# Copying gate matrices out of PSUM on VectorE instead of ScalarE after the last selection, with the gates' pace counted for it

## The chip, the cores and the metric

The kernel runs on one NeuronCore of a Trainium2 chip. Its five engines (TensorE, VectorE, ScalarE, GpSimd and SyncE, in the profile PE, DVE, ACT, POOL and SP) each work through a queue of their own in order and wait for one another by semaphores. The metric is the device time of one execution in microseconds (us), lower is better.

## The reference

One layer of a diffusion backbone over 512 latent tokens and 256 context tokens, D = 1024. The mixers come first; the part that matters here is the feed-forward at the end, PEER, in which each token retrieves 128 of 16384 one-neuron experts (8 heads, 16 each):

```python
half_s, half_i = lax.top_k(s, PEER_TOPK)               # scores against two sets of 128 keys
cand = half_s[:, :, 0, :, None] + half_s[:, :, 1, None, :]
best_s, best_c = lax.top_k(cand.reshape(...), PEER_TOPK)
experts = i1 * PEER_KEYS + i2
gate = jax.nn.softmax(best_s, axis=-1)
act = jax.nn.gelu(jnp.einsum('td,thkd->thk', hb, u_table[experts]))
return jnp.einsum('thk,thkd->td', gate * act, v_table[experts])
```

## The kernel before, in words

For 384 of the 512 tokens PEER is computed densely: all 16384 experts are taken in 128 blocks of 128. The *first product* of a block (`first_product`, 24 matmuls of 384 columns, tile `pa`) gives the activations of its experts for all 384 tokens, and the *second product* (18 matmuls of 512 columns, tiles `pacc`) adds activation times gate times v. The remaining 128 tokens gather their own rows of u and v (`gather_u`, `gather_v`): GpSimd fetches 128 rows of 4 KB at a time into `grow`, VectorE takes a dot product of it (L1452).

The dense gates must be built: `gate_matrices` makes, for four tokens at a time (a *set*), one-hot matrices on VectorE (`h1` at L1429, `o2` at L1431), scales `h1` by the gate on ScalarE (`o1`, four ACTIVATE at L1433), multiplies them on TensorE into a PSUM tile `pm` (L1439), and copies that into `stg` (L1440), whose token index is the innermost one: the copy reads `pm` in a row and writes elements that lie 32 floats, 128 bytes, apart. There are 96 sets; eight fill one `stg`, and a full `stg` is written to `Gd` in DRAM by four DMAs that ScalarE's queue issues (L1445). Matmul and copy of a set stand two sets behind its one-hots (`GLAG = 2`); `pm` has two buffers.

The stage in question is a loop over blocks (`while nb < NBLK and (not gm.done or nb % GRP)`). One iteration transposes the u of the block two further on (`transpose_u`: DVE L1486, ACT cast `w_hi` L1487, POOL `w_lo` in two halves L1491), issues a first product, writes its activations to `Ad` in DRAM, and then runs three side programs by budgets in us: gathers, gate matrices (`gm`) and selections (`tk`, one for each 128 tokens). A side program gets its budget added to what it is owed, and runs pieces until their `yield`s have used it up; `spent` counts the work handed out. Once the three selections are done (`tk.done`), `stage[0]` becomes 1 and the gates' budget per block becomes `GMX`. The loop ends at the first multiple of 4 blocks at which all 96 sets are done: 112 here. The other 16 blocks go through a *second loop* over turns n = 0 to 132: there a turn does the first product of a block that is left (if one is) and, five turns behind, the second product of a block; blocks that went through the first loop come last there and read `Ad` back. `Gd` is read in groups of eight blocks (`gg`).

The orders of VectorE and GpSimd are those of the program text (`manual_schedule`); TensorE, ScalarE and SyncE are ordered by a scheduler when the kernel is built. Iterations and blocks are counted from 0 below, sets from 1; iteration i of the first loop opens with the transpose for block i + 2, written T(i + 2).

Of the kernel before, what the change touches and what calls it, by code (L numbers as in the profile page):

```python
# [55 lines left out]
TK0 = 10  # L56
TK1 = 30
SLACK = 10
GMX = 3.3
GU2 = 1.6  # L60
TKORD = [0, 1, 2]
PRI = 3000
# [73 lines left out]
def body(ctx: ExitStack, tc: tile.TileContext, I, out, dbg=lambda *a: None):  # L136
    nc = tc.nc
    V, S, G, PE, SP = nc.vector, nc.scalar, nc.gpsimd, nc.tensor, nc.sync
# [56 lines left out]
    def psum(tag="a", name="pt"):  # L195
        return ps.tile([P, 512], F32, name=name, tag=tag, bufs={"a": 2, "s": 3, "o": 1}[tag])
# [49 lines left out]
    pt = psum()  # L246
    PE.transpose(pt[:, :16], crow2, ident[:16, :16])
    V.tensor_copy(vcol[:, :16], pt[:, :16])
    pt = psum()
# [30 lines left out]
    for k in range(KC):  # L280
        for i in range(3):
            if i % 2 == 0:
                pt = psum("as"[n // 2 % 2])
# [105 lines left out]
    pt = psum()  # L389
# [686 lines left out]
    ready, now, spent, stage = {}, [0], [0.0, 0.0], [0]  # L1076
# [148 lines left out]
    for h in range(4):  # L1225
        szh = gate_tile(16 + h)
        pt = psum()
# [15 lines left out]
    for h0 in range(0, HEADS, 4):  # L1243
        pt = psum()
# [156 lines left out]
    def pkt(shape, name, dt=F32, bufs=1):  # L1401
        return pk.tile(shape, dt, name=name, tag=name, bufs=bufs)
# [13 lines left out]
    def gate_matrices(l):  # L1416

        while l not in ready or now[0] < ready[l][0] + MWAIT:
            yield 0.0
        i1, i2, gT = ready[l][1:]  # L1420
        held = []
        for t0 in range(0, P, TB):
            stg = pkt([P, KEYS, TB], "stg", bufs=2)
            for t in range(t0, t0 + TB + 4 * GLAG, 4):
                busy = t < t0 + TB
                if busy:
                    if t % OT == 0:
                        h1 = pkt([P, P, OT], "h1", BF, bufs=GLAG + 1)
                        V.tensor_tensor(h1, iotab, i1[:, None, t:t + OT].to_broadcast([P, P, OT]), op=ALU.is_equal)  # L1429
                    o2, o1 = pkt([P, 4, P], "o2", bufs=GLAG + 1), pkt([P, 4, P], "o1", bufs=GLAG + 1)  # L1430
                    V.tensor_tensor(o2, io[0][:, None, :].to_broadcast([P, 4, P]), i2[:, t:t + 4, None].to_broadcast([P, 4, P]), op=ALU.is_equal)  # L1431
                    for j in range(4):
                        S.activation(o1[:, j], h1[:, :, t % OT + j], AF.Copy, scale=gT[:, t + j:t + j + 1])  # L1433
                    held.append((t, o1, o2))
                if len(held) > GLAG or not busy:
                    tp, o1, o2 = held.pop(0)
                    pt = ps.tile([P, 512], F32, name="pm", tag="m", bufs=2)
                    for j in range(4):
                        PE.matmul(pt[:, j * P:(j + 1) * P], o2[:, j], o1[:, j], start=True, stop=True)  # L1439
                    S.copy(stg[:, :, tp - t0:tp - t0 + 4].rearrange("p i t -> p t i"), pt.rearrange("p (t i) -> p t i", t=4))  # L1440
                    spent[0] += 0.9
                yield 1.1 if busy else 0.01
            pc = (l * P + t0) // TB
            for i0 in range(0, KEYS, 32):
                S.dma_start(Gd[pc, :, i0:i0 + 32], stg[:, i0:i0 + 32])  # L1445
# [32 lines left out]
    def transpose_u(b):  # L1478
# [13 lines left out]
        return tuple(x.rearrange("p (k f) -> p k f", f=P) for x in (hi, lo))  # L1492

    gm = Side(chain(gate_matrices(0), gate_matrices(1), gate_matrices(2)))
    spent[:] = [0.0, 0.0]
    gu = Side(chain(gather_u(), gather_v()))
# [11 lines left out]
    while nb < NBLK and (not gm.done or nb % GRP):  # L1508
# [13 lines left out]
        if tk.done and not stage[0]:  # L1522
            stage[0] = 1
        gm.run(GM if not tk.done else GMX)
        if not tk.done:
# [166 lines left out]
```

## Time and profile before

| | |
|---|---|
| median of three runs | 2057.54 us (2054.82 to 2059.9) |
| the profiled execution: time, span | 2055.5 us, 2053.7 us |
| TensorE (matmul) busy over the span | 1912.8 us, 93% |
| VectorE busy | 1637.4 us, 80% |
| ScalarE busy | 951.4 us, 46% |
| GpSimd busy | 978.9 us, 48% |
| granted TensorE clock, mean | 0.975 of full speed |

Shares over the whole span are means over very different stages: the mixers fill the first 790 us, the first loop runs from there to some 1417 us, the second to the end. A stage is read by its own rows. A time such as 1304.76 is counted from the start of the span.

### The profile page before, as it was taken

The numbers are of one execution on the slowest core, as the hardware profiler recorded it, in microseconds if no ns is written. First come the engines' busy times: TensorE is split into PE (matmuls) and PEld (weight loads), VectorE is DVE, ScalarE is ACT, GpSimd is POOL, SyncE is SP. The second block draws the span as 40 slices with busy tenths as digits, with TensorE's granted clock in tenths as the row PEclk, the third lists the DMA queues.
The fourth block names the chain that finished last, engine by engine and source line by source line (L and its number), as shares of the span: only waits on it lengthen the run. The fifth ranks groups of instructions, "written<-read, shape, count | busy, mean of one in ns | idle before, by whom it ended". The sixth has DMA issues, their size and how long they took to land.

```text
span 2053.7 us, 29600 instructions
## 1 busy us (share of the span) xinstructions
PE 1912.8 (93%) x10018; PEld 1622.3 (79%) x10018; DVE 1637.4 (80%) x3311; ACT 951.4 (46%) x1770; POOL 978.9 (48%) x695
## 2 busy tenths in 40 slices
PE   7999999999898997999999999989889999999997
PEld 2766667788786796889999999889777888888885
DVE  4599885377766659899998999666779888989886
ACT  4455554333332443333666666797323333333333
POOL 2755444311212872677666566443345545545430
PEclk9999999999999998999999999999999999999999
DMA  9333332422425785889888888788999999999992
GB/s 311 93 113 109 109 92 83 128 84 62 125 68 175 214 199 157 240 234 257 246 248 261 248 249 247 228 280 286 300 311 356 390 357 399 381 379 380 393 389 87
DMA packets 283477, 475.87 MB, mean 232 GB/s; under 512 B 35224, under 2 KB 197293, under 8 KB 282813
## 3 DMA queue, kind: packets, MB, share of 16 engines
q1 hardware_dynamic: 214251, 277.82, 44.5%
q0 software_dynamic: 36864, 134.23, 19.2%
q10 hardware_dynamic: 32210, 61.93, 8.4%
q8 instruction: 79, 1.29, 0.3%
q14 instruction: 73, 0.60, 0.1%
HBM read 409.71 MB, written 64.18 MB: 231 GB/s over the span
## 4 chain that ended last, share of the span: by engine, by line
PE 37%; POOL 9%; DMA 6%; issue 6%; ACT 6%; DVE 4%; ACTq 1%; SPq 1%; DVEq 0%; POOLq 0%
PE pacc L174 8%; PE pacc L175 8%; PE pacc L173 8%; POOL w_lo L1491 6%; PE pa L175 3%; PE pa L173 3%; PE pa L174 3%; DMA w_raw<-in_peer_u_dram 3%; ACT o L1433 2%; ACT stg L1440 2%; PE pm L1439 2%; POOL grow L1459 2%; POOL w_lo L169 1%; ACT w_hi L1487 1%; DMA w_raw<-in_peer_wq_dram 1%
## 5 line engine op out<-in xcount | busy, mean ns | idle before, releaser
L1491 POOL TENSOR_TENSOR w_lo<-ut,w_hi 128x512 fp32r<-128x512 f32 x224 | 294.6, 1338 | 229.0 <-ACT w_hi L1487 223.3
L173 PE MATMUL pa<-h2T_hi,w_hi 128*128 128x384 f32 x1024 | 355.5, 347 | 38.9 <-ACT w_hi L1487 36.1
L175 PE MATMUL pa<-h2T_hi,w_lo 128*128 128x384 f32 x1024 | 360.0, 353 | 8.5 <-POOL w_lo L1491 6.9
L174 PE MATMUL pa<-h2T_lo,w_hi 128*128 128x384 f32 x1024 | 349.7, 341 | 0.0
L169 POOL TENSOR_TENSOR w_lo<-w_raw,w_hi 128x1024 fp32r<-128x1024 f32 x78 | 198.5, 2557 | 301.7 <-ACT w_hi L168 222.0
L1470 POOL DMA_INDIRECT grow<-in_peer_v_dram,exi x128 | 205.0, 1601 | 211.6 <-DVE accg L1474 190.1
L1573 ACT CAST w_hi<-w_raw 128x1024 fp32r<-128x1024 f32 x124 | 130.5, 1053 | 244.7 <-PE pacc L175 89.2
L173 PEld LDWEIGHTS pa<-h2T_hi,w_hi 128*128 128x128 f32 x1024 | 198.1, 193 | 46.6 <-ACT w_hi L1487 46.1
L175 PEld LDWEIGHTS pa<-h2T_hi,w_lo 128*128 128x128 f32 x1024 | 197.8, 193 | 14.5 <-POOL w_lo L1491 11.1
L174 PE MATMUL pacc<-w_lo,wh 128*128 128x512 f32 x744 | 194.6, 396 | 9.2 <-DVE w_lo L1577 9.2
L1459 POOL DMA_INDIRECT grow<-in_peer_u_dram,exi x128 | 148.6, 1161 | 104.8 <-DVE act L1452 85.2
L174 PEld LDWEIGHTS pa<-h2T_lo,w_hi 128*128 128x128 f32 x1024 | 197.6, 193 | 0.3
L175 PE MATMUL pacc<-w_hi,wl 128*128 128x512 f32 x744 | 193.7, 395 | 0.0
L173 PE MATMUL pacc<-w_hi,wh 128*128 128x512 f32 x744 | 193.7, 395 | 0.0
L1487 ACT CAST w_hi<-ut 128x1024 fp32r<-128x1024 f32 x126 | 132.4, 1052 | 131.1 <-DVE ut L1486 105.0
L174 PEld LDWEIGHTS pacc<-w_lo,wh 128*128 128x128 f32 x744 | 139.0, 188 | 44.9 <-DVE w_lo L1577 12.0
L1577 DVE TENSOR_TENSOR w_lo<-w_raw,w_hi 128x1024 fp32r<-128x1024 f32 x124 | 151.3, 1220 | 22.9 <-ACT w_hi L1573 22.8
L175 PEld LDWEIGHTS pacc<-w_hi,wl 128*128 128x128 f32 x744 | 139.7, 188 | 33.9
L173 PEld LDWEIGHTS pacc<-w_hi,wh 128*128 128x128 f32 x744 | 139.6, 188 | 33.9
L1486 DVE STREAM_TRANSPOSE ut<-w_raw 128x1024 f32<-128x1024 f32 x126 | 155.6, 1237 | 12.6 <-DMA w_raw<-in_peer_u_dram 10.7
L1474 DVE SCALAR_TENSOR_TENSOR accg<-grow,act,accg 128x1024 f32<-128x1024 f32 x127 | 162.4, 1279 | 3.2 <-DMA grow<-in_peer_v_dram,exi 2.2
L173 PE MATMUL pg<-hL_hi,w_hi 128*128 128x512 f32 (+1 forms) x336 | 139.7, 416 | 0.0
(450 smaller groups left out, 4092.9 us busy)
## 6 DMA issues: line engine op xcount, KB each, us to landing
w_raw<-in_peer_u_dram SPq DMA_DIRECT2D x512, 128.0 KB
w_raw<-in_peer_v_dram SPq DMA_DIRECT2D x128, 512.0 KB
Gd<-stg ACTq DMA_DIRECT2D x48, 512.0 KB
gg<-Gd SPq DMA_DIRECT2D x16, 1536.0 KB
Ad<-ga ACTq DMA_DIRECT2D x112, 192.0 KB
aa<-Ad SPq DMA_DIRECT2D x28, 768.0 KB
w_raw<-in_w_ada_dram SPq DMA_DIRECT2D x40, 512.0 KB
w_raw<-in_w_in_dram SPq DMA_DIRECT2D x34, 512.0 KB
```

The source lines that it names most:

```text
L169: (lo_eng or G).tensor_tensor(lo, raw, hi.bitcast(F32), op=ALU.subtract)
L173: PE.matmul(o, lh, rh, start=start, stop=False)
L174: PE.matmul(o, lh, rl, start=False, stop=False)
L175: PE.matmul(o, ll, rh, start=False, stop=stop)
L1459: G.indirect_dma_start(out=u, out_offset=None, in_=UT_, in_offset=bass.IndirectOffsetOnAxis(ap=exi[:, j:j + 1], axis=0))
L1470: G.indirect_dma_start(out=v, out_offset=None, in_=VT_, in_offset=bass.IndirectOffsetOnAxis(ap=exi[:, j:j + 1], axis=0))
L1474: V.scalar_tensor_tensor(accg, v, act[:, j:j + 1], accg, op0=ALU.mult, op1=ALU.add)
L1486: V.transpose(lf.rearrange("p (c f q) -> p c f q", f=4, q=32), u.rearrange("p f (c x) -> p c f x", x=32))
L1487: S.copy(hi, lf)
L1491: eng.tensor_tensor(lo[:, cs], lf[:, cs], hi[:, cs].bitcast(F32), op=ALU.subtract)
L1573: S.copy(vh, v)
L1577: V.tensor_tensor(vl, v, vh.bitcast(F32), op=ALU.subtract)
```

## The change

Once the last selection is done, VectorE's `tensor_copy` takes the place of ScalarE's `copy` for a set, and a set's `yield` is 1.7 (before 1.1), a copy without new one-hots 0.6 (before 0.01). The budget for each block becomes 4.4 (before 3.3).

```diff
-GMX = 3.3
+GMX = 4.4
...
-                    S.copy(stg[:, :, tp - t0:tp - t0 + 4].rearrange("p i t -> p t i"), pt.rearrange("p (t i) -> p t i", t=4))
+                    (V.tensor_copy if stage[0] else S.copy)(stg[:, :, tp - t0:tp - t0 + 4].rearrange("p i t -> p t i"),
+                                                            pt.rearrange("p (t i) -> p t i", t=4))
                     spent[0] += 0.9
-                yield 1.1 if busy else 0.01
+                yield (1.7 if stage[0] else 1.1) if busy else 0.6 if stage[0] else 0.01
```

What the planner makes of it: sets 55 to 96 are copied by VectorE, 42 in all. Eight sets now use 14.8 us of budget, that is 3.4 blocks, where they used 8.8 us or 2.7 blocks. All sets are done at block 116, not 112, so 116 blocks pass through the first loop and 12 are left to the second, where it was 112 and 16; and the first group that the second loop reads from `Gd` has four blocks (0.75 MB), not eight (1.5 MB).

VectorE's order in an iteration late in the first loop, before. `ut` is the transpose, the two ISA rows are one dot product and its sum, `h1` and `o2` the one-hots:

```order
L1486 STREAM_TRANSPOSE ut_13146<-w_raw_13139 128x1024
L1452 ISA grow_12995,act_6998<-grow_12995,h2p_7008 128x1024
L1452 ISA act_6998 128x1
L1429 TENSOR_TENSOR h1_13182<-iop_7010,i1_12584 128x512
L1431 TENSOR_TENSOR o2_13184<-iop_7010,i2_12585 128x512
L1429 TENSOR_TENSOR h1_13197<-iop_7010,i1_12584 128x512
L1431 TENSOR_TENSOR o2_13199<-iop_7010,i2_12585 128x512
L1429 TENSOR_TENSOR h1_13212<-iop_7010,i1_12584 128x512
L1431 TENSOR_TENSOR o2_13214<-iop_7010,i2_12585 128x512
L1486 STREAM_TRANSPOSE ut_13234<-w_raw_13227 128x1024
```

And now, the end of iteration 104 (its transpose and two dots stand ahead; `pm_13199` is set 72, the last of a `stg`, and `pm_13237` is set 73) and the start of iteration 105:

```order
L1453 ISA act_6998 128x1
L1440 COPY stg_12906<-pm_13199 128x4x128
L1429 TENSOR_TENSOR h1_13210<-iop_7010,i1_12584 128x512
L1431 TENSOR_TENSOR o2_13212<-iop_7010,i2_12585 128x512
L1429 TENSOR_TENSOR h1_13219<-iop_7010,i1_12584 128x512
L1431 TENSOR_TENSOR o2_13221<-iop_7010,i2_12585 128x512
L1429 TENSOR_TENSOR h1_13228<-iop_7010,i1_12584 128x512
L1431 TENSOR_TENSOR o2_13230<-iop_7010,i2_12585 128x512
L1440 COPY stg_13209<-pm_13237 128x4x128
L1487 STREAM_TRANSPOSE ut_13250<-w_raw_13243 128x1024
```

The copies stand between the one-hots, and the next block's transpose now stands behind a copy, which waits for a matmul.

TensorE's order around the copies of sets 73 to 75, now. `pa_13328` is the first product of block 106, whose transpose opened iteration 104, and `pa_13416` that of block 107:

```order
L174 MATMUL pa_13328<-h2T_lo_5733,w_hi_13158 128x384
L175 MATMUL pa_13328<-h2T_hi_5732,w_lo_13159 128x384
L173 MATMUL pa_13328<-h2T_hi_5732,w_hi_13158 128x384
L174 MATMUL pa_13328<-h2T_lo_5733,w_hi_13158 128x384
L175 MATMUL pa_13328<-h2T_hi_5732,w_lo_13159 128x384
L1439 MATMUL pm_13237<-o1_13213,o2_13212 128x128 x4
L1439 MATMUL pm_13295<-o1_13222,o2_13221 128x128 x4
L1439 MATMUL pm_13310<-o1_13231,o2_13230 128x128 x4
L173 MATMUL pa_13416<-h2T_hi_5732,w_hi_13248 128x384
```

Before (`pa_13239` is block 104, whose transpose opened iteration 102, `pa_13330` block 105; the sets 73 and 74 were made in iteration 102):

```order
L173 MATMUL pa_13239<-h2T_hi_5732,w_hi_13051 128x384
L174 MATMUL pa_13239<-h2T_lo_5733,w_hi_13051 128x384
L175 MATMUL pa_13239<-h2T_hi_5732,w_lo_13052 128x384
L1439 MATMUL pm_13191<-o1_13124,o2_13123 128x128 x4
L173 MATMUL pa_13330<-h2T_hi_5732,w_hi_13144 128x384
L174 MATMUL pa_13330<-h2T_lo_5733,w_hi_13144 128x384
L1439 MATMUL pm_13206<-o1_13133,o2_13132 128x128 x4
L175 MATMUL pa_13330<-h2T_hi_5732,w_lo_13145 128x384
```

In both, the matmul of set 73 stands behind the whole first product of the block whose transpose opened the iteration that makes set 73. Before, VectorE first waited for that matmul in the next iteration (the one-hot of set 76 takes the buffer of set 73); now the copy of set 73 waits for it in the same one.

ScalarE's order at the same place, now: the four stores of a full `stg` stand ahead of the scalings of sets 73 to 75, and those ahead of the cast for block 107:

```order
L1514 ACTIVATE ga1_13280<-pa_13255 128x384
L1515 DMA Ad26_6986<-ga1_13280 128x384
L1446 DMA Gd_6959<-stg_12906 128x1024 x4
L1433 ACTIVATE o1_13213<-h1_13210,gT_12581 128x128 x4
L1433 ACTIVATE o1_13222<-h1_13219,gT_12581 128x128 x4
L1433 ACTIVATE o1_13231<-h1_13228,gT_12581 128x128 x4
L1514 ACTIVATE ga1_13353<-pa_13328 128x384
L1515 DMA Ad26_6986<-ga1_13353 128x384
L1488 CAST w_hi_13248<-ut_13250 128x1024
```

Before, the copies stood among them:

```order
L1445 DMA Gd_6959<-stg_12863 128x1024 x4
L1440 COPY stg_13120<-pm_13191 128x4x128
L1433 ACTIVATE o1_13200<-h1_13197,gT_12581 128x128 x4
L1440 COPY stg_13120<-pm_13206 128x4x128
L1433 ACTIVATE o1_13215<-h1_13212,gT_12581 128x128 x4
L1514 DMA Ad26_6986<-ga1_13264 128x384
L1487 CAST w_hi_13232<-ut_13234 128x1024
```

On ScalarE the copies are gone and everything else has moved up.

## Rows read from the trace of the kernel before

**Rows 1.** Windows of 50 us around the first loop's end: busy us of each engine, PEclk, DMA

```profile
1250.00:1300.00 50.00, 49.96 (x312) 49.29 (x310) 40.56 (x59) 35.41 (x64) 31.05 (x26) 1.00 0.86 250
1300.00:1350.00 50.00, 43.61 (x277) 41.28 (x277) 37.00 (x64) 43.37 (x100) 22.74 (x20) 0.97 0.83 258
1350.00:1400.00 50.00, 44.57 (x289) 42.56 (x287) 33.97 (x58) 43.58 (x98) 22.74 (x20) 0.97 0.84 260
...
1550.00:1600.00 50.00, 50.00 (x216) 40.21 (x215) 45.72 (x71) 18.37 (x25) 26.60 (x17) 1.00 1.00 363
```

**Rows 2.** Groups by line, 1304 to 1418 us: busy, mean ns, idle before and releaser

```profile
L1433 ACT ACTIVATE o<-h,gT 128x128 f32<-128x128 bf16 x160 | 52.4, 418 | 0.0
L1440 ACT COPY stg<-pm 128x512 f32<-128x512 f32 x40 | 43.9, 1097 | 10.0 <-DMA w_raw<-in_peer_u_dram 4.3 <-PE pm L1439 3.6 <-issue 2.1
L1487 ACT CAST w_hi<-ut 128x1024 fp32r<-128x1024 f32 x16 | 17.0, 1061 | 3.1 <-DVE o L1431 3.1
...
L1431 DVE TENSOR_TENSOR o<-iop,i 128x512 f32<-128x512 f32 x38 | 26.1, 687 | 32.6 <-PE pm L1439 31.6 <-issue 0.9
...
L1439 PE MATMUL pm<-o,o 128*128 128x128 f32 x320 | 44.6, 282 | 6.6 <-ACT stg L1440 6.6
```

**Rows 3.** Timeline of DVE: start, us, what, idle before

```profile
1304.76 1.23 DVE L1486 STREAM_TRANSPOSE ut<-w_raw 128x1024 f32<-128x1024 f32 x1
1305.91 1.18 DVE L1452 CUSTOM_DVE_ANT_0 grow<-grow,h2p 128x1024 f32<-128x1024 f32 x1
...
1307.03 1.21 DVE L1452 CUSTOM_DVE_ANT_0 grow<-grow,h2p 128x1024 f32<-128x1024 f32 x1
...
1316.50 0.42 DVE L1429 TENSOR_TENSOR h<-iop,i 128x512 bf16<-128x512 bf16 x1
1316.84 0.68 DVE L1431 TENSOR_TENSOR o<-iop,i 128x512 f32<-128x512 f32 x1
1317.44 0.41 DVE L1429 TENSOR_TENSOR h<-iop,i 128x512 bf16<-128x512 bf16 x1
```

**Rows 4.** Timeline of PE, ACT and POOL late in the first loop

```profile
1410.88 1.16 PE L1439 MATMUL pm<-o,o 128*128 128x128 f32 x8 [0.36 <-ACT stg L1440]
1411.79 0.42 PE L175 MATMUL pa<-h2T_hi,w_lo 128*128 128x384 f32 x1
...
1418.00 0.33 PE L175 MATMUL pa<-h2T_hi,w_lo 128*128 128x384 f32 x1
...
1420.08 0.33 PE L175 MATMUL pa<-h2T_hi,w_lo 128*128 128x384 f32 x1
...
1300.00 3.06 ACTq L1445 DMA_DIRECT2D Gd<-stg  x4
...
1415.88 1.16 ACT L1440 COPY stg<-pm 128x512 f32<-128x512 f32 x1
...
1318.49 2.53 POOL L1491 TENSOR_TENSOR w_lo<-ut,w_hi 128x512 fp32r<-128x512 f32 x2 [4.46 <-ACT w_hi L1487]
```

**Rows 5.** Groups by line and form over the whole span: other copies and reads

```profile
L1358 ACT COPY sce<-pt 128x512 f32<-128x512 f32 x16 | 9.4, 587 | 4.3 <-PE pt L1356 3.3 <-DMA scd<-sce 0.9
...
L651 DVE COPY mid<-pt 128x512 f32<-128x512 f32 x16 | 10.8, 676 | 1.5 <-PE pt L649 1.5
...
L624 DVE TENSOR_REDUCE mx<-pt 128x1 f32<-128x256 f32 x16 | 6.5, 409 | 0.0
L810 DVE TENSOR_REDUCE Ac<-ods 128x32 f32<-128x256 f32 x6 | 3.5, 591 | 0.1
```

**Rows 6.** The second loop's start: chain that ended last, DVE, and SP's u loads

```profile
1419.02 13.40 DMA Gd<-stg
...
1439.71 0.56 DVE L1562 TENSOR_TENSOR ga<-gg,ga 128x384 f32<-128x384 f32 x1 [6.44 <-DMA gg<-Gd]
...
1454.54 1.74 SPq L1482 DMA_DIRECT2D w_raw<-in_peer_u_dram  x4
...
1510.64 1.75 SPq L1482 DMA_DIRECT2D w_raw<-in_peer_u_dram  x4
```

## What the change should do

> **What bounds the kernel now.** I read the windows of the span first. Ahead of the last selection TensorE is busy for 49.96 of 50 us; from 1300 to 1400 us it is busy for 88.2 of 100 while ScalarE's 35 us in 50 rise to 43; from 1550 us on TensorE is full again [rows 1]. So the change can gain only in the last 14 blocks of the first loop and at the start of the second. The groups of that stretch say who holds whom: ScalarE never waits long (scaling 52.4 us, copies 43.9, casts 17.0, which with the activations and the stores' issue fills the 114 us), VectorE waits 31.6 us for TensorE's gate matmuls, and TensorE waits for ScalarE's copies and casts [rows 2]. ScalarE is the bound there. TensorE's own work would need less: 12 matmuls of a first product take 2.08 us, so 24 take 4.16, and a set's matmuls take 0.91 [rows 4]; 14 blocks and 40 sets come to 58.2 + 36.4 = 95 us, and the stretch lasts from T(100), which opens iteration 98 at 1304.76 [rows 3], to the end of the last copy at 1415.88 + 1.16 = 1417.04 [rows 4].
>
> **The price of one copy on VectorE.** ScalarE's copy into `stg` takes 1097 ns [rows 2]; its copy of the same 128x512 from PSUM to elements in a row takes 587, so the 128-byte step costs it 510 ns [rows 5]. VectorE's copy in a row takes 676 ns; no row shows it writing with such a step. The nearest is a sum that reads with a step of 64 bytes: 591 ns for 256 elements where a sum over 256 in a row takes 409, 0.71 ns more for each element [rows 5]. On 512 elements that makes 676 + 364 = 1040 ns. Below, a step that costs nothing when written leaves 676; above, ScalarE's own surcharge makes 676 + 510 = 1186. I take 1.04 to 1.1, since two rows of two engines show that a step costs. An instruction follows its predecessor about 0.08 us before that one's recorded end (a transpose of 1.23 us is followed after 1.15, a one-hot `o2` of 0.68 after 0.60 [rows 3]), so a copy occupies VectorE for c = 1.0 (0.6 to 1.1).
>
> [...]
>
> **VectorE in the longer stretch.** The first loop now runs to block 116. From iteration 98 to 115 VectorE has 18 transposes of 1.15, 24 dots of 1.12 and 38 sets of 0.34 + 0.60 [rows 3]: 20.7 + 26.9 + 35.7 = 83.3 us, and 40 copies of c = 1.0, so 123.3. TensorE needs 18 x 4.16 + 40 x 0.91 = 111.3 in the same stretch, ScalarE 40 x 4 scalings at 0.33 (52.4 / 160), 18 casts of 1.06 and five groups of stores of 3.06, 87, beside the short activations. VectorE takes ScalarE's place as the bound.
>
> **The new wait.** Copies now stand in VectorE's order, and the next transpose behind them. I walked the 18 iterations by hand with these durations, in the orders that the changed program has. Iteration 104 as the example, from its start: transpose to 1.15, two dots to 3.4, copy 72 to 4.4, then three sets to 7.2. Copy 73 needs the matmul behind block 106, whose transpose opened the iteration: transpose 1.15, cast 1.06 [rows 2], first half of `w_lo` 1.26 [rows 4], 24 matmuls 4.16, so 7.6; but its scaling stands on ScalarE behind the four stores, which wait for copy 72 and take 3.06 [rows 4]: 4.4 + 3.1 + 1.3 = 8.8, the matmul ends at 9.7, and copy 73 waits 2.5 us. Of this kind I find nine waits: about 1.0 in iteration 98, 2.0 in 100, 1.8 in 101, 1.1 in 103, 2.5 in 104, 2.3 in 109, 2.4 in 110, 1.5 in 112, 1.9 in 113: 16.5 in all. Where an iteration has fewer sets or its matmul belongs to the block before, there is none. Behind each waiting copy stand the next transpose and one-hots, and TensorE waits for those next. If copies are cheaper, these waits grow by about half of what is saved: at c = 0.6 they come to some 22.5, at 1.1 to 15.
>
> **The sum to the end of the first loop.** Iteration 97 gets two copies more and one set less, 1.1 us. T(100) then stands at 1305.9; plus 83.3, 40 and 16.5 is 1445.7; the last copy ends a transpose and a dot earlier, at 1443.4. That is 26.4 us later than 1417.0.
>
> **What comes back in the second loop.** There are four blocks fewer. A turn with a first and a second product takes (1510.64 - 1454.54) / 6 = 9.35 us, seven loads of u being six turns [rows 6]; a turn with a second product alone takes 50 x 18 / 216 = 4.17 [rows 1]. Four turns change kind: 4 x 5.18 = 20.7 us back. What starts the second loop does not change in kind: the last `stg` is stored (13.40 us), `gg` is read, and VectorE waits 6.44 us for it [rows 6]; the first group is half as large, which I take at 1.5 us (between 0 and half of the wait, 3.2, since the next group and the u loads are behind it in the same queue). TensorE has five blocks left at that point and hides under the same wait. The Ad stores and reads of four more blocks, 0.75 MB each way, fall where TensorE is full, with fewer gathers left over; I cost them at nothing, and if the DMA engines' full share there [rows 1] turned them into a wait, 0.75 MB at the 363 GB/s of that window would be 2 us.
>
> Sum: +26.4 - 20.7 - 1.5 = +4.2. What the walk leaves out (GpSimd's gathers ahead of `w_lo`, the stores of activations on ScalarE's queue) I put at +2, from 0 to 5. So +6 us on the profiled execution's 2055.5: **2062 us**; that execution lies 2 us under the median of the runs shown. 0.3%, about what a measurement of this kernel can tell from no change, is 6.2 us, so the forecast lies on that edge, and its own range is +0.5 to +12, 2056 to 2068.
>
> **Rivals.**
> *The step costs nothing when written.* c = 0.6: 83.3 + 24 + 22.5 from 1305.1, the last copy ends at 1432.6, +15.6 - 22.2 + 2 = -5: 2051. For it: the 676 ns. Against: both rows with a step.
> *Faster: the waits aren't there.* TensorE could be ahead of VectorE more than my walk says, since each wait hangs on one cast's place on ScalarE, which is freed of 1.1 us for every copy. With c = 1.0 and no waits the last copy ends at 1426.9: +9.9 - 22.2 = -12: 2043. It decides once the waits sum to less than about 12 us. Against it: before, VectorE already waited 31.6 us for just these matmuls [rows 2], one iteration later in its order.
> *Slower: in lockstep.* VectorE, ScalarE and TensorE wait on each other in turn, c is 1.1 and each of the 18 iterations loses 1.4 us, 25 in all: 1306.1 + 83.3 + 44 + 25 - 2.3 = 1456.1, +39.1 - 22.2 + 2 = +19: 2074. For it: the queue positions shown above; a late copy delays the transpose, the transpose the cast, the cast the block, the block the next copy. Against: half of the iterations have slack.
> *It does nothing.* If the bound were TensorE all along, the pace alone would shift four blocks from one loop to the other: 0 to 3 us, 2057. Against: TensorE's 11.8 idle us in 100.
>
> **How the numbers follow.** The forecast gets 0.43 (of that 0.25 under 6.2 us and 0.18 over), the free step 0.17 (0.12 within, 0.05 faster), no waits 0.13, lockstep 0.22, nothing 0.05. Faster: 0.05 + 0.13 = 0.18; same: 0.25 + 0.12 + 0.05 = 0.42; slower: 0.18 + 0.22 = 0.40. The range reaches to the other cases: 2047 leaves out most of the rival without waits, 2075 the tail of lockstep.
>
> **What would show it.** The copy's mean on VectorE (1.04 to 1.2 us, or 0.68); VectorE over 85% busy between 1310 and 1440 and waiting for `pm` at the copies, in bursts of 1 to 3 us; ScalarE under 70%; the last copy at 1440 to 1447; seven turns of some 9.3 us after that. It is wrong if the copy is cheap, if VectorE's waits at copies sum to under 10 or over 22 us, or if a turn with both products gets shorter or longer because fewer gathers or a smaller `gg` change what it waits for.

## The result and the profile after

| | before | after |
|---|---|---|
| median of 13 runs | 2060.79 us (2054.82 to 2070.73) | 2082.99 us (2066.47 to 2092.17) |
| ratio | | 1.0091, interval 1.0074 to 1.0108 |
| profiled execution: span | 2053.7 us | 2088.9 us |

By the ratio the change makes the kernel slower by 19 us; the medians lie 22 us apart. The forecast was 2062 us, and its range ended at 2075.

The two programs have the same order of instructions up to the last selection, so the 17 us by which T(99) is already later in the profile of the changed kernel, called after here (1316.61 against 1299.68), are not the change's. From T(99) to the end of the span it is 772.3 us against 754.0, 18.3 more, about what the ratio gives. All that follows counts from T(99), about where the change sets in, and cuts the rest at L, the end of the last copy, and F, the end of the last first product's last matmul.

The windows of after that answer to [rows 1], and two short ones at the start of the second loop (busy us of PE, PEld, DVE, ACT, POOL; PEclk, DMA share, GB/s):

```profile
1300.00:1350.00 50.00, 43.85 (x272) 41.97 (x271) 38.94 (x62) 27.72 (x64) 24.46 (x21) 1.00 0.78 237
1350.00:1400.00 50.00, 43.93 (x260) 41.45 (x261) 41.76 (x66) 29.04 (x76) 22.82 (x20) 0.93 0.74 239
1400.00:1450.00 50.00, 42.03 (x253) 40.60 (x253) 43.08 (x66) 26.56 (x69) 22.88 (x20) 0.93 0.81 255
...
1480.00:1490.00 10.00, 10.00 (x58) 9.82 (x57) 5.49 (x9) 3.90 (x6) 3.56 (x3) 1.00 1.09 360
1490.00:1500.00 10.00, 4.17 (x24) 3.73 (x22) 0.24 (x1) 0.00 (x0) 0.00 (x0) 0.81 1.04 293
```

ScalarE has room now, busy for some 28 of 50 us, but TensorE is no busier than before. The groups from T(99) to L say why, against [rows 2]:

```profile
L1440 DVE COPY stg<-pm 128x512 f32<-128x512 f32 x42 | 45.0, 1087 | 20.0 <-PE pm L1439 19.9
...
L1431 DVE TENSOR_TENSOR o<-iop,i 128x512 f32<-128x512 f32 x40 | 27.2, 680 | 0.0
...
L175 PE MATMUL pa<-h2T_hi,w_lo 128*128 128x384 f32 x137 | 50.0, 365 | 5.8 <-POOL w_lo L1492 5.8
L173 PE MATMUL pa<-h2T_hi,w_hi 128*128 128x384 f32 x138 | 49.5, 358 | 7.2 <-ACT w_hi L1488 7.2
L1439 PE MATMUL pm<-o,o 128*128 128x128 f32 x328 | 48.2, 293 | 9.5 <-ACT o L1433 8.4 <-DVE stg L1440 0.9
...
L1433 ACT ACTIVATE o<-h,gT 128x128 f32<-128x128 bf16 x160 | 51.7, 401 | 35.4 <-DMA Gd<-stg 12.6 <-DVE h L1429 7.6 <-DVE ut L1487 4.8
```

VectorE's waits have moved from the one-hots to the copies, and outside of them it does not idle at all. Its timeline, where the prediction named rows (start, us, what, idle before):

```profile
1322.53 1.25 DVE L1487 STREAM_TRANSPOSE ut<-w_raw 128x1024 f32<-128x1024 f32 x1
...
1378.76 0.42 DVE L1429 TENSOR_TENSOR h<-iop,i 128x512 bf16<-128x512 bf16 x1
...
1383.74 1.06 DVE L1440 COPY stg<-pm 128x512 f32<-128x512 f32 x1 [2.11 <-PE pm L1439]
1384.64 1.22 DVE L1487 STREAM_TRANSPOSE ut<-w_raw 128x1024 f32<-128x1024 f32 x1
...
1460.71 1.06 DVE L1440 COPY stg<-pm 128x512 f32<-128x512 f32 x1
...
1463.87 1.24 DVE L1487 STREAM_TRANSPOSE ut<-w_raw 128x1024 f32<-128x1024 f32 x1
...
1483.09 0.56 DVE L1563 TENSOR_TENSOR ga<-gg,ga 128x384 f32<-128x384 f32 x1 [0.40 <-DMA gg<-Gd]
...
1499.76 1.25 DVE L1487 STREAM_TRANSPOSE ut<-w_raw 128x1024 f32<-128x1024 f32 x1 [12.68 <-DMA w_raw<-in_peer_u_dram]
```

The first row is T(100). Copy 73 (1383.74) waits 2.1 us, and the transpose goes behind it; the last copy ends at 1461.77, 2.1 us ahead of T(118), which opens the second loop. At the start of the second loop `gg` is hardly waited for, but T(123) waits 12.68 us for its u, and TensorE is busy for 4.17 of 10 us. SyncE's queue has that u load (1482.38) behind the two reads of `Gd` and the two of `Ad`:

```profile
1473.82 3.53 SPq L1549 DMA_DIRECT2D gg<-Gd  x2
1477.41 4.88 SPq L1553 DMA_DIRECT2D aa<-Ad  x2
1482.38 1.80 SPq L1483 DMA_DIRECT2D w_raw<-in_peer_u_dram  x4
```

Before, the first u of this kind (block 119) stood ahead of them. So the sum can be taken in TensorE's time, from T(99) to L, F, 1850 us and the end. Before:

```profile
1299.68:1417.04 117.36, 103.71 (x664) 98.44 (x663) 81.83 (x138) 104.27 (x231) 55.60 (x49) 0.97 0.84 262
1417.04:1534.24 117.20, 104.82 (x510) 94.18 (x509) 85.82 (x113) 35.46 (x48) 42.92 (x31) 0.96 0.99 309
1534.24:1850.00 315.76, 313.55 (x1344) 251.93 (x1344) 275.44 (x345) 115.11 (x154) 161.26 (x100) 1.00 0.99 375
1850.00:2053.70 203.70, 189.59 (x812) 151.89 (x810) 168.36 (x214) 71.32 (x107) 66.14 (x45) 0.98 0.82 314
sum 754.02, PE 711.67 PEld 596.43 DVE 611.46 ACT 326.16 POOL 325.93; mean PE 177.92 PEld 149.11 DVE 152.86 ACT 81.54 POOL 81.48
```

After:

```profile
1316.61:1461.77 145.16, 122.24 (x741) 116.02 (x739) 125.15 (x190) 77.00 (x196) 65.98 (x58) 0.95 0.77 244
1461.77:1550.33 88.56, 74.68 (x365) 68.47 (x366) 57.82 (x75) 25.50 (x34) 33.67 (x24) 0.90 0.95 299
1550.33:1850.00 299.67, 295.51 (x1259) 235.41 (x1259) 261.58 (x334) 109.00 (x145) 162.28 (x94) 1.00 0.99 370
1850.00:2088.90 238.90, 226.22 (x969) 181.36 (x967) 198.65 (x249) 85.06 (x124) 88.70 (x56) 0.98 0.87 331
sum 772.29, PE 718.66 PEld 601.26 DVE 643.20 ACT 296.57 POOL 350.63; mean PE 179.66 PEld 150.32 DVE 160.80 ACT 74.14 POOL 87.66
```

TensorE has the same matmuls in both. It idles 53.6 us now and 42.3 before: 11.3 us, of which 9.3 (22.9 against 13.6) lie ahead of L. It is busy 7.0 us longer for the same work, where the granted clock is 0.95 and 0.90 against 0.97 and 0.96. Together these are the 18.3.

L is not the same place of the program in every kernel. Of first products, 24 matmuls each, the traces have 357 matmuls behind L before, 286 in after, 278 in e2 and 164 in e8 below: by L, 3.0 blocks have moved ahead in after, 3.3 in e2 and 8.0 in e8, where the first loop takes 4, 4 and 12 blocks more.

### The profile page after: what moved, and what is told of

Read it like the earlier page. It is cut to its first block, busy times and chain, and to the rows that moved or that the text cites. A ratio compares the mean times of both kernels' runs of the same rounds, so it can differ in the third digit from the quotient of the medians.

```text
span 2088.9 us, 29591 instructions
## 1 busy us (share of the span) xinstructions
PE 1930.8 (92%) x10018; PEld 1633.4 (78%) x10018; DVE 1676.1 (80%) x3349; ACT 921.9 (44%) x1728; POOL 1007.2 (48%) x703
## 2 busy tenths in 40 slices
DMA packets 285748, 478.22 MB, mean 229 GB/s; under 512 B 35320, under 2 KB 199437, under 8 KB 285085
## 3 DMA queue, kind: packets, MB, share of 16 engines
q1 hardware_dynamic: 215947, 279.39, 43.7%
## 4 chain that ended last, share of the span: by engine, by line
PE 30%; issue 14%; POOL 13%; DMA 6%; DVE 5%; ACT 1%; SPq 0%; ACTq 0%; DVEq 0%; POOLq 0%
POOL w_lo L1492 8%; PE pacc L174 5%; PE pacc L175 5%; PE pacc L173 5%; PE pa L175 3%; DMA aa<-Ad 3%; PE pa L173 3%; PE pa L174 3%; POOL grow L1460 3%; PE pm L1439 2%; POOL w_lo L169 2%; DVE w_lo L1578 1%; DVE accg L1475 1%; DMA w_raw<-in_peer_wq_dram 1%; PE pt L175 1%
## 5 line engine op out<-in xcount | busy, mean ns | idle before, releaser
L1492 POOL TENSOR_TENSOR w_lo<-ut,w_hi 128x512 fp32r<-128x512 f32 x232 | 306.2, 1343 | 252.9 <-ACT w_hi L1488 244.8
L1471 POOL DMA_INDIRECT grow<-in_peer_v_dram,exi x128 | 219.3, 1713 | 199.7 <-DVE accg L1475 183.5
L175 PEld LDWEIGHTS pa<-h2T_hi,w_lo 128*128 128x128 f32 x1024 | 198.8, 194 | 21.8 <-POOL w_lo L1492 19.8
L1433 ACT ACTIVATE o<-h,gT 128x128 f32<-128x128 bf16 x384 | 126.0, 403 | 49.0 <-DMA Gd<-stg 15.1
```

The source lines that it names most:

```text
L175: PE.matmul(o, ll, rh, start=False, stop=stop)
L1471: G.indirect_dma_start(out=v, out_offset=None, in_=VT_, in_offset=bass.IndirectOffsetOnAxis(ap=exi[:, j:j + 1], axis=0))
L1492: eng.tensor_tensor(lo[:, cs], lf[:, cs], hi[:, cs].bitcast(F32), op=ALU.subtract)
```

## The experiments

Ratios are to the kernel before, with 95% intervals; the times are of the profiled executions.

| kernel | ratio | T(99) to L | L to F | F to end | T(99) to end |
|---|---|---|---|---|---|
| before | 1 | 117.4 | 117.2 | 519.5 | 754.0 |
| after | 1.0091 (1.0074 to 1.0108) | 145.2 | 88.6 | 538.6 | 772.3 |
| e1 u load moved | 1.0056 (1.0034 to 1.0078) | 145.4 | 87.3 | 532.0 | 764.7 |
| e2 pace alone | 0.9941 (0.9921 to 0.9961) | 121.9 | 85.2 | 537.4 | 744.4 |
| e3 copies alone | 1.0134 (1.0111 to 1.0157) | 138.2 | 125.4 | 520.3 | 783.9 |
| e4 copy in a row | 1.0005 (0.9986 to 1.0025) | 134.4 | 84.5 | 538.1 | 757.1 |
| e5 pace, u load moved | 0.9975 (0.9952 to 0.9997) | 120.8 | 83.6 | 543.1 | 747.5 |
| e6 copy a set later | 1.0062 (1.0038 to 1.0086) | 143.3 | 87.7 | 539.1 | 770.1 |
| e7 every second copy | 1.0002 (0.9983 to 1.0021) | 129.6 | 89.3 | 532.8 | 751.7 |
| e8 pace, 124 blocks | 0.9928 (0.9905 to 0.9950) | 141.0 | 28.6 | 563.1 | 732.7 |
| e9 gathers held back | 1.0064 (1.0039 to 1.0089) | 145.6 | 78.6 | 548.6 | 772.8 |
| e10 pace, gathers held | 0.9951 (0.9934 to 0.9969) | 121.5 | 75.6 | 548.8 | 745.9 |
| e11 stores on SyncE | 1.0045 (1.0027 to 1.0062) | 138.4 | 90.8 | 539.5 | 768.7 |
| e12 half of the v loads | 1.0026 (1.0008 to 1.0044) | 145.7 | 85.9 | 531.5 | 763.1 |

### The first four: the load, the pace, the copies, their step

**e1.** In the turn that reads the first `Gd` group:

```diff
+            if n == SKEW:
+                early_u[b + 1] = load_u(b + 1)
+                early_v[ORDER[0]] = load_v(ORDER[0])
+                early_u[b + 2] = load_u(b + 2, G)
```

> The changed kernel, but at the first turn of the second loop the u of the next-but-one block (123) is loaded from GpSimd's queue, and the u of the next block and the first v are issued ahead of the two reads of Gd on SyncE's queue. Theory A (of the 19 us, some 12 are lost because that u load stands on SyncE's queue behind two reads that wait for the last store of a stg): VectorE's wait of 12.68 us before T(123) shrinks to under 2, the time falls by 8 to 13 us to a ratio of 1.003 to 1.005 against the kernel before. Rival B (all of the 19 us is the lock-step of the copies in VectorE's order): no change, ratio 1.008 to 1.010. Rival C (the load is late because the stores and reads fill the DMA engines, not for its place in the queue): T(123) stays at 35 to 40 us behind the last copy, ratio 1.008 to 1.010.

VectorE's wait before T(123) is gone: T(123) starts 9.8 us behind T(122), where after had 20.7. But the next one, whose u is now the first behind the reads, starts 17.5 us later:

```profile
1480.28 1.24 DVE L1498 STREAM_TRANSPOSE ut<-w_raw 128x1024 f32<-128x1024 f32 x1
1497.77 1.25 DVE L1498 STREAM_TRANSPOSE ut<-w_raw 128x1024 f32<-128x1024 f32 x1 [4.39 <-DMA w_raw<-in_peer_u_dram]
```

L to F is 1.3 us shorter, not 8 to 13. The profile's other 6.6 us come after F, where nothing was changed. Theory A is mostly wrong.

**e2.** The kernel before with the change's `yield` and `GMX` lines, and `S.copy` kept.

> The kernel before with the new yields and the new GMX, copies still on ScalarE; 116 blocks in the first loop, and the u load of block 123 behind the reads of Gd as in the changed kernel. ScalarE has 18 casts, 160 scalings and 40 copies, so the last copy comes 5 to 12 us later than before, not 28. Theory A: the hole before T(123) is there as well (8 to 13 us), and four turns give 17 back: +8 - 10, ratio 0.997 to 1.002. Rival B: no hole; +8 - 21, ratio 0.993 to 0.995.

The pace alone is faster than before. Three blocks more cost 4.5 us ahead of L (121.9 against 117.4), about what ScalarE's busy time grew (104.3 to 108.9):

```profile
1307.86:1429.76 121.90, 115.42 (x743) 111.31 (x742) 89.73 (x151) 108.93 (x238) 67.67 (x60) 0.97 0.92 289
```

TensorE idles 6.5 us in it, where before had 13.6: the blocks went in good part into idle time. L to the end is 14.1 us shorter. So the change is a gain of 12 us by pace and a loss of some 30 by its copies.

**e3.** The change's copy line alone, with the old pace.

> VectorE copies, but with the old yields and the old GMX; 112 blocks in the first loop. VectorE has 118.7 us of work in iterations 98 to 111 (14 x 1.15 + 24 x 1.12 + 38 x 0.94 + 40 x 1.0) where the stretch took 112, and waits. Theory A: the last copy 20 to 30 us later than before, a hole before T(119) on top, nothing given back by the turns: ratio 1.012 to 1.020. Rival B: the same lock-step without the hole, ratio 1.008 to 1.013. If copies off ScalarE let TensorE run ahead, as the rival without waits had it, 1.000 to 1.004.

As theory A had it in size, and 20.9 us of it lie ahead of L. L to F is 8.2 longer than before, with the same 16 blocks left to the second loop.

**e4.** `stg` as `[P, TB, KEYS]`, and the copy:

```diff
+                    (V.tensor_copy if stage[0] else S.copy)(stg[:, tp - t0:tp - t0 + 4], pt.rearrange("p (t i) -> p t i", t=4))
```

> The changed kernel with stg laid out token by token, so that the copy writes elements in a row; the gates then stand in Gd in another order than the reference's, everything else is the same work. Theory (the step of 128 bytes costs VectorE 0.41 us a copy): copies take 0.68 us, the last copy ends 8 to 16 us earlier than in the changed kernel (16 saved, up to half of it taken back by longer waits), ratio 1.001 to 1.006. Rival (the lock-step with TensorE and ScalarE sets the pace, the copy's own length does not): copies take 0.68 us, waits grow by the same, ratio 1.008 to 1.010.

```profile
L1440 DVE COPY stg<-pm 128x512 f32<-128x512 f32 x42 | 28.6, 686 | 23.0 <-PE pm L1439 22.9
```

The step costs 401 ns a copy, 16.4 us over 42. T(99) to L falls by 10.8, and waits grow by 3. So the length of the copy, not only its place, sets the pace.

### The second four: where a copy hurts, and how far the pace carries

**e5.** e2 with the edit of e1.

> The pace alone (copies on ScalarE, 116 blocks) with the u load of block 123 on GpSimd's queue and that of block 122 ahead of the reads of Gd. If a load's place behind the reads of Gd costs what the same edit gave back in the changed kernel (7.6 us from T(99) to the end), the ratio falls from 0.994 to 0.989 to 0.992. If that was chance, or the DMA engines, full in that stretch, set the time whatever the order, it stays at 0.992 to 0.996.

L to F is 1.5 us shorter than in e2, much as in e1, and the whole is not faster than e2. The order of the loads is worth 1 to 2 us, and what e1 had beyond that was not repeated.

**e6.** Each copy leaves a list one set later than its matmul:

```diff
+                    pend.append((stg, tp - t0, pt, (l * P + t0) // TB))
+                    if len(pend) > (1 if stage[0] else 0):
+                        copy_out(*pend.pop(0))
```

> The changed kernel with each VectorE copy written one set later than its matmul (the copies' number, length and engine are the same, and so are the pace and the u loads). Theory (lock-step: the copy stands in VectorE's order before TensorE can have made its matrix): the waits at copies fall from 20 us to under 8, T(99) to the last copy from 145 to 130 to 136 us, ratio 1.002 to 1.005. Rival (the length of 40 copies and ScalarE's stores, which wait for a copy, set the pace): the stretch stays at 141 to 147, ratio 1.007 to 1.010.

```profile
L1419 DVE COPY stg<-pm 128x512 f32<-128x512 f32 x42 | 45.0, 1083 | 10.7 <-PE pm L1447 10.7
...
L1439 DVE TENSOR_TENSOR o<-iop,i 128x512 f32<-128x512 f32 x40 | 27.3, 683 | 7.7 <-PE pm L1447 7.7
```

Nine us of waits left the copies, and 7.7 came back at the one-hots, which wait for the same matmuls. The stretch is 1.9 us shorter, against 9 to 15 expected: the place of a copy by one set does not matter here, with two `pm` buffers, and the theory falls in that form. Whether it would with more buffers was not tried.

**e7.** `V.tensor_copy if stage[0] and tp % 8 else S.copy`.

> The changed kernel with every second copy back on ScalarE: 20 copies, 21.8 us, on VectorE. With all copies on ScalarE T(99) to the last copy took 121.8 us, with all on VectorE 145.2. If the cost goes by the copy: 133, ratio near 1.001. If any copy in VectorE's order puts the engines in lock-step: 140 or more, ratio 1.005 or more. If VectorE has room for 20: 121 to 127, ratio 0.994 to 0.997.

T(99) to L is 129.6: the first 21 copies cost 7.7 us more than none (e2), the other 21 another 15.6. VectorE has some room, and then none. Between the cases expected, nearer to the cost by the copy.

**e8.** e2 with `GMX = 3.3`, and so 124 blocks in the first loop.

> The pace alone with the old budget of 3.3 and the new yields: 124 blocks go through the first loop, copies on ScalarE. If the first loop has idle TensorE time to fill and is TensorE's after that, 26 x 4.16 + 36.4 = 145 us and some 6 idle from T(100) to the last copy, 33 us more than before; twelve turns with one product less give up to 62 back, of which the start of the second loop keeps some 12: ratio 0.988 to 0.994. If the start of the second loop is bound by its DMA (the reads of Gd and Ad), there is no more than with 116 blocks: 0.994 to 0.998.

```profile
1305.23:1446.20 140.97, 133.02 (x857) 130.59 (x856) 104.82 (x170) 117.47 (x248) 89.26 (x79) 0.99 0.99 305
1446.20:1474.80 28.60, 28.60 (x167) 28.60 (x166) 13.62 (x18) 9.44 (x14) 14.45 (x13) 1.00 1.05 379
```

The best kernel of the study, about as fast as e2 by the intervals. Eight blocks more ahead of L cost 23.6 us there and shorten the rest from 636.7 to 591.7, 5.6 us a block. That is more than the 4.16 us of a block's matmuls: TensorE's idle time from L on falls too, from 28.7 to 21.8 us, and from L to F there is none.

### The last four: what sets the second loop

From L to 1850 us the DMA engines are 0.95 busy or more in all kernels so far, and share times length, from T(99) to the end, came to 694 to 704 us in each of them. So they were suspected of setting the time.

**e9, e10.** After and e2 with the second loop's gathers held back:

```diff
-            if part:
+            if part and n >= NBLK - nb:
```

> The changed kernel, with the gathers of the second loop held back until its last first product is issued (turn 12): the same gathers, spread over the later turns. In the changed kernel the last copy to the end of the last first product (L to F) takes 88.6 us, in which the DMA engines are 0.95 busy and move 26.5 MB; TensorE has 75 us of work there at its lower clock. If the DMA engines set that stretch, some 9 MB less make L to F 62 to 75 us. If it is the place or the latency of single loads, the hole before T(123) stays over 8 us and L to F at 82 to 90. The time of the whole: if DMA is the bound up to 1850 us as well, F to the end grows by 15 to 25 and the ratio stays at 1.006 to 1.012; if TensorE is the bound from F on, the ratio falls to 1.000 to 1.004.

> The same hold on the gathers in the pace-alone kernel, where L to F takes 85.1 us. If DMA sets that stretch: L to F 60 to 72. If DMA is the bound after it too: ratio 0.992 to 0.997, as the pace alone; if TensorE is: 0.984 to 0.989.

L to F fell by 10.0 and 9.6 us, less than the DMA case had it, and F to the end grew by 10.0 and 11.4. The hole before T(123) shrank from 20.7 to 17.4 behind T(122). DMA traffic does press on the start (the DMA share from L to F is 0.80 and 0.81 here, 0.95 and 1.00 in after and e2), but moving it gains nothing that these runs can tell.

**e11.** `(SP if stage[0] else S).dma_start(Gd...)`.

> The changed kernel with the four stores of a full stg issued by SyncE's queue and not ScalarE's, after the last selection. The prediction's example had scalings standing behind these stores, which wait for a VectorE copy: ScalarE is idle 12.6 us there between T(99) and the last copy, and TensorE waits 8.4 us for scaled one-hots. If this queueing makes the waits at copies: they fall from 20 to 12 to 16 us, the stretch from 145 to 138 to 142, ratio 1.004 to 1.007. If the copies wait for the block's matmuls anyway, or u loads queue behind the stores on SyncE instead: 144 to 148, ratio 1.008 to 1.011.

```profile
L1440 DVE COPY stg<-pm 128x512 f32<-128x512 f32 x42 | 45.2, 1087 | 13.3 <-PE pm L1439 13.3
```

As the first theory had it: scalings no longer stand behind stores that wait for a copy, TensorE's wait for `o1` falls from 8.4 to 2.4 us, and 6.8 of the lost us come back ahead of L; 2.2 are lost again from L to F, which was not looked into.

**e12.** In the second loop, until 16 blocks are left:

```diff
+        if n % 2 == 0 or n >= NBLK - 16:
+            vt[0] = raw_tile()
+            SP.dma_start(vt[0], VT_[b * P:(b + 1) * P])
+        v = vt[0]
```

> The changed kernel, but in the second loop 56 of the 128 loads of v are left out and the product takes the v of the block before (so its outputs aren't the reference's); TensorE, VectorE and ScalarE do the same work. From T(99) to the end the twelve kernels so far had 694 to 704 us of DMA time (share of the windows times their length), and what differed was the unused rest. 56 loads of 0.52 MB are 29 MB, about 80 us at the 0.36 MB per us of that stretch. If the DMA engines set the second loop: the last copy to the end falls from 627 us by 25 to 75, to where TensorE's own 600 us bound it or below, ratio 0.975 to 0.997. If TensorE, busy all of 1550 to 1850 us, sets it: the last copy to the end stays within 8 us, ratio 1.005 to 1.010, and the DMA share falls to 0.85 or so.

```profile
1536.40:1850.00 313.60, 312.19 (x1338) 250.68 (x1337) 280.68 (x353) 111.67 (x154) 128.34 (x100) 1.00 0.90 319
1850.00:2067.90 217.90, 207.68 (x891) 166.73 (x889) 182.06 (x230) 75.92 (x114) 59.61 (x50) 0.98 0.79 283
```

With 29 MB less the DMA share from F to 1850 us falls from 0.99 to 0.90, and L to the end by 9.7 us, where the DMA theory asked for 25 at least and the rival for 8 at most; by the ratios, 1.0026 against 1.0091, it is 13. TensorE stays full (312.19 of 313.60 us from F to 1850), so it sets the second loop from F on; these loads add some 10 us to it. That the DMA time was about equal in all kernels did not show a bound: they move nearly the same data (over the whole span 475.87 MB before, 478.22 MB in after).

## Why the prediction was wrong

**Price of a copy: right.** 1.04 to 1.1 us was predicted for the mean, 1.087 measured. It occupies VectorE for 0.90 (1383.74 to 1384.64), where c = 1.0 was taken. e4 gives the step alone: 686 ns in a row, where 676 was taken, and 401 ns for the step, where 364 was worked out from the two sums.

**The first loop: right.** VectorE's 83.3 + 40 + 16.5 = 139.8 us from T(100) to T(118) measured 141.3 (1322.53 to 1463.87). Waits at copies were 20.0, with shorter copies to make up for it. The worked example holds: copy 73 waits 2.1 us for 2.5, and e11, which takes the stores from in front of its scalings, removes a third of all waits. T(99) to L is 27.8 us longer, where the sum had 26.4 and 2 for what the walk leaves out, from 0 to 5. That waits grow by half of what shorter copies save was too much: e4 saved 16.4 and the waits grew by 3.

**The failed step: what comes back in the second loop.** "Four turns change kind: 4 x 5.18 = 20.7 us back", and 1.5 for `gg`, were set against "26.4 us later than 1417.0" for the last copy. This is where the miss of some 12 us arose, in two parts.

First, the two terms do not meet at one place. Before, the second loop opens with T(114), and the last copy ends 4.5 us behind it, at 1417.04; now the last copy ends ahead of T(118), as the walk had it. Before and after, cut at T(114) and T(118):

```profile
1412.49 1.25 DVE L1486 STREAM_TRANSPOSE ut<-w_raw 128x1024 f32<-128x1024 f32 x1 [0.64 <-POOL w_lo L1491]
...
1299.68:1412.49 112.81, 99.16 (x635) 93.89 (x634) 79.62 (x137) 99.72 (x227) 51.48 (x45) 0.97 0.84 263
1412.49:2053.70 641.21, 612.51 (x2692) 502.55 (x2690) 531.84 (x671) 226.44 (x312) 274.45 (x177) 0.99 0.94 343
...
1316.61:1463.87 147.26, 123.95 (x746) 117.72 (x745) 127.25 (x193) 77.00 (x196) 67.94 (x60) 0.95 0.77 245
1463.87:2088.90 625.03, 594.71 (x2586) 483.54 (x2585) 515.95 (x655) 219.56 (x301) 282.69 (x171) 0.98 0.94 345
```

The second loop opens 34.5 us later, counted from T(99). The walk itself had 33.2 (1445.7 against 1412.5), but the sum took the 26.4 between the last copies, between which only three blocks change sides, together with what four blocks give back. That is 6.8 us too few.

Second, the price. The second loop lasts 625.0 us where it lasted 641.2: 16.2 us back, not 22.2. The price was read from seven turns at the start of the second loop, where TensorE also waits: 9.35 us, of which 4.17 + 4.16 are its matmuls. From T(114) and T(118) on, TensorE's busy time falls by 17.8 us, and its idle time rises from 28.7 to 30.3: the four blocks took their matmuls with them and none of the waits. In e8 some of the waits go as well, and twelve blocks give back 64.8 us (576.4 from T(126)), 5.4 each. So 5.18 is near the mark where waits go with the turns, and was too much for these four. This second part is less sure: from T(118) to the end, kernels with 116 blocks in the first loop and all their loads take 617 to 628 us in single profiles, 13 to 24 less than before.

**What else stands in these 6 us.** "What starts the second loop does not change in kind" was wrong of SyncE's queue, where the u load of T(123) has come to stand behind the reads of `Gd`, but e1 and e5 price that at 1.3 and 1.5 us. The granted clock is another term that the sum did not have: from L to F it is 0.90 in after, e1 and e3, which have VectorE copies, 0.94 in e4, whose VectorE copies are shorter, and 0.94 to 0.96 in before, e2 and e5. F to the end varies from 532 to 543 us among kernels that are the same from there on, so the last few us of one profile can't be assigned.

**The rivals.** "In lockstep" came nearest in time, but not by its mechanism: it had the last copy 39 us later. "No waits" fell with the 20 us. "It does nothing" was wrong about pace, which it took to be worth 0 to 3 us: e2 gains 12. That does not speak against the forecast's bound: in e2 ScalarE is busy for 108.9 of 121.9 us, and the stretch grows as its work does. The two halves of the change should have been priced apart.

## What to carry to other kernels

When work moves from one stage to another, price it by the bounding engine's own time, not by the length of a turn that holds waits; the waits come back only if they go too. Let the term for one stage end where the term for the next begins. Price a change of engine and a change of pace apart, since one can hide the other's sign. A resource that is full and has the same total in every variant isn't thereby the bound: take some of its load away and see.

## What the runs showed of the hardware

VectorE's copy of 128x512 floats out of PSUM takes 686 ns when it writes in a row (e4) and 1087 when the elements lie 128 bytes apart (after). ScalarE's two forms differ by 510 ns [rows 2, 5]: in this kernel the step is dear on both engines, and changing the engine did not avoid it.

In after and e3 TensorE idles more than before, and the same matmuls take longer; in e8 it idles less, and they take less. In after the wait at a copy in iteration 101 is 4.62 us where 1.8 was worked out. Four windows of after lead up to it (columns as above):

```profile
1345.00:1350.00 5.00, 2.65 (x18) 2.33 (x17) 4.08 (x5) 0.02 (x1) 0.00 (x0) 1.00 0.79 274
1350.00:1355.00 5.00, 3.37 (x14) 2.86 (x15) 4.96 (x11) 4.60 (x13) 2.56 (x3) 0.79 1.03 351
1355.00:1359.00 4.00, 4.00 (x16) 4.00 (x16) 0.00 (x0) 1.75 (x6) 1.86 (x2) 0.50 0.74 217
1360.00:1365.00 5.00, 4.35 (x31) 4.04 (x30) 5.00 (x9) 2.75 (x6) 2.11 (x2) 1.00 0.39 119
```

TensorE idled for 2.35 of the first 5 us and 1.63 of the next, and the granted clock was 1.00 and then 0.79; from 1355 to 1359 it was 0.50, while VectorE waited for TensorE, busy for none of 4 us. From 1360 to 1365 it is 1.00 again. Whether the idling lowers the clock, or both have another cause, is not shown. Over T(99) to the end the same matmuls took 7.0 us more of TensorE's time than before. e3, which idles most ahead of F (43.7 us, before 26.0), took 13.0 more, at a granted clock of 0.91 and 0.90 there; e8, which idles least (8.0), took 8.8 less, at 0.99 and 1.00.

A u load of 0.5 MB issued at 1482.38 was there for T(123) at 1499.76, 17 us later, with the DMA engines at 1.09 and 1.04 in those windows.
